# An encoder trunk on one core: first bias sums in a free buffer, later bias loads behind the stacks, gates stored through GpSimd's queue

## The chip, the core and the metric

The kernel runs on one core of one Trainium2 chip. A core has TensorE (matmuls, PE in the profile, with its weight loads as PEld), VectorE (DVE), ScalarE (ACT), GpSimd (POOL) and SyncE (SP, which only starts transfers). The metric is the device time of one execution in microseconds; the time of a kernel is the median of several runs.

## The reference

Two layers of an encoder over 512 tokens of width 1024. Each layer is a feed-forward half-step, a mixer with three attention branches, and a second feed-forward half-step. The change lies in the mixer:

```python
u = rmsnorm(h, mix_pre_g[l])
proj = u @ w_in[l]
qa, ka, va, qb, kb, vb, qc, kc, vc, gl = jnp.split(proj, split_at, axis=-1)
oa = neighbourhood_attention(qa, ka, va, na_rpb[l])          # branch A, 8 heads
ob = sliding_window_attention(qb, kb, vb, sw_sink[l])        # branch B, 8 heads, 2 key heads
oc = differential_attention(qc, kc, vc, lam, lam_init, ...)  # branch C, 4 heads
yb = jnp.einsum('bsnc,ncd->bsnd', stack([oa, ob, oc]), w_branch[l])
gates = jax.nn.sigmoid(gl.reshape(b, s, 3, D_MODEL) + b_gate[l])
merged = jnp.sum(gates * yb, axis=2)
h = h + rmsnorm(merged @ w_out[l], mix_post_g[l])
```

In branch A each head has its own table of biases by relative position, which are added to the scores, and a mask for the columns outside the window:

```python
bias = rpb[:, dr[:, None, :, None], dc[None, :, None, :]]
scores = scores + bias[None].astype(jnp.float32)
scores = jnp.where(col_ok[None, None, None, :, None, :], scores, NEG)
p = jax.nn.softmax(scores.reshape(b, h, rows, GRID_W, kr * GRID_W), axis=-1)
```

## The kernel before

All is float32. Matmuls are done on operands split into a high and a low part, three matmuls for a product. A layer has four phases, each with a pool of SBUF tiles of its own: feed-forward, projection (`project`), mixer (`mixer`), feed-forward. The pools of consecutive phases use the same memory, so a tile of the mixer's pool can be written when the projection's tiles under it are done with. Other tiles live in a pool for the whole program (`sb`), with a fixed number of buffers for each tag: the tag `n` has two buffers of 128 x 2048 floats.

`project` computes the queries, keys and values. Most of them it stores to DRAM as high and low parts (`part`, `store`, line 1405, on GpSimd's queue); those of the first pair of heads of branch A stay in SBUF, in tiles named `early`. In its loop over groups, at group 6, it calls `tables_of_a`: the three masks of branch A and the bias tables of heads 0 and 1 are loaded into one buffer of the tag `n`, the tile `pre`. The other buffer of that tag is then free until the first gates.

`mixer` works through steps that the text `ORDER` names, in that order:

- `qa0` to `qa3` load what a pair of heads of branch A needs (`qkv_a`). `ask` starts the load of a head's bias table (`braw`, line 1726; nothing to load for heads 0 and 1). `restacked` starts 12 loads of 128 KB that put high and low parts of queries and keys on top of each other (`st`, lines 1776 and 1777), and `values` two loads of values (`x`, line 1753). All are on SyncE's queue.
- `aa0` to `aa3` are the attention of such a pair (`attn_a`). For each head, `biases` adds the mask to shifted views of the bias table, four additions on VectorE (line 1737), into two tiles, `bedge` and `bmid`, of the mixer's tag `g`, which has ten buffers. `softmax_pv` computes the scores (line 1672), adds the bias and takes the maximum in one operation of VectorE (line 1675), takes the exponential (line 1684) and scales (line 1692) on ScalarE, transposes (line 1703), splits the result (lines 352 and 353) and multiplies it with the values (lines 1706 and 1707).
- `kb`, `qb`, `ab` and `qc`, `ac`, `fc` are the loads and attention of branches B and C.
- `ga`, `gb`, `gc` with a number 0 to 7 each compute 128 of 1024 gates of a branch: 24 matmuls (lines 326 to 328) and a tanh (line 1909). Gates of branch A stay in SBUF, four in one buffer of the tag `n`; the first four take the buffer that is free beside `pre`, the next four that of `pre`. Gates of B and C go through two buffers of the tag `gd` and are stored to DRAM (line 1912, SyncE's queue).
- `ya`, `yb`, `yc` multiply a branch with its output weights and apply the gate (`combine`): gates of B are loaded back into `gd` buffers, the product with the gate is line 1922 on VectorE, the sum over branches line 1926, for branch B on GpSimd.

Weights come in blocks of 512 KB (`wr`, line 211), whose loads ScalarE starts in the mixer, and are split into high and low parts on ScalarE and VectorE (lines 224 and 225). Two PSUM banks (`mm`) take the products of gates and combine steps in turn.

Outside some regions that are ordered by hand, a scheduler lays down each engine's instructions when the program is built: it goes by the order in which the steps are written and by modelled times, and it picks which buffer of a tag a tile gets. On the chip each engine and each queue then works strictly in that order; whoever must wait holds up all that stands behind it.

Of the kernel before, what the change touches and what calls it, by code (L numbers as in the profile page):

```python
# [10 lines left out]
F32 = mybir.dt.float32  # L11
# [5 lines left out]
P = 128  # L17
# [3 lines left out]
T = 512  # L21
# [18 lines left out]
QA, KA, VA, QB, KB, VB, QC, KC, VC, GL = 0, 4, 8, 12, 16, 17, 18, 22, 26, 30  # L40
# [29 lines left out]


ORDER = """
qa0 qa1 aa0 ga0 ga1 qa2 aa1 ga2 qa3 aa2 ga3 gb0 kb qb0 aa3 gb1 qb1 ab0
gb2 gb3 qb2 ab1 gb4 gb5 gb6 qb3 ab2 gb7 ga4 qc0 ab3 ga5 ga6 qc1 ac0
ga7 ya0 gc0 ya1 qc2 fc0 ac1 gc1 ya2 gc2 ya3 gc3 fc1 qc3 ac2 ya4 ya5
ya6 ya7 yb0 gc4 fc2 ac3 yb1 gc5 yb2 gc6 fc3 yb3 gc7 yb4 yb5 yb6 yb7
yc0 yc1 yc2 yc3 yc4 yc5 yc6 yc7
# [42 lines left out]
def encoder_kernel(ctx: ExitStack, tc: tile.TileContext, order, xT, wts, cols, rows, rpb, consts, tables, out):  # L120
    nc = tc.nc
# [3 lines left out]
    sb = ctx.enter_context(tc.tile_pool(name="sb", bufs=1))  # L125
# [4 lines left out]
    BUFS = {"X": 6, "n": 2, "wr": 3, "wp": 2, "wq": 2}  # L130
# [16 lines left out]
    def nm(s):  # L147
        serial[0] += 1
        return f"{s}{serial[0]}"

    def big(tag, dt=F32, shape=(P, T), name="v"):
        if tag in BUFS:
            return sb.tile(list(shape), dt, tag=tag, name=nm(name), bufs=BUFS[tag])
        kind, pool = phase[0]
        return pool.tile(list(shape), dt, tag=tag, name=nm(name), bufs=ABUFS[kind][tag])
# [7 lines left out]
    V, A, G, PE = nc.vector, nc.scalar, nc.gpsimd, nc.tensor  # L163

    def f(t):
        return t.bitcast(F32)
# [15 lines left out]
    def col(name, l, b=0, t=None):  # L182
        c = COLS[name, l] + b
        return (colt if t is None else t)[:, c : c + 1]
# [76 lines left out]
    for l in range(L):  # L261
        for which in (1, 2):
            name = f"ffn{which}_w_down"
# [81 lines left out]
    def dense1(name, l, c, X, r0=0, tag="mm", midway=None):  # L345
        return dense([(name, l, r0, c)], X, (tag,), midway=midway)[0]
# [1021 lines left out]
    def project(l, op, accs):  # L1368
# [112 lines left out]
        made = {}  # L1481
# [38 lines left out]
        for n, c0 in (("cosR", 0), ("sinR", 512)):  # L1520
            t = big("rr", name=n)
# [25 lines left out]
        def tables_of_a():  # L1547
            t = sb.tile([P, 4, T], F32, tag="n", name=nm("pre"), bufs=BUFS["n"])
            nc.sync.dma_start(t[:, 0, :], tables[:, 1024 : 1024 + 512])
            nc.sync.dma_start(t[:, 1, :256], tables[:, 1024 + 512 : 1024 + 768])  # L1550
            for hd in range(2):
                nc.sync.dma_start(t[:, 2 + hd, :], raw_of(l, hd))
            made["tables"] = t

        def gate_tile(c):
            if (c - GL) % 4 == 0:
                made["gates"].append(sb.tile([P, 4, T], F32, tag="n", name=nm("gate"), bufs=BUFS["n"]))
            return made["gates"][-1][:, (c - GL) % 4, :]
# [19 lines left out]
        for g in range(count):  # L1578
# [48 lines left out]
            if g == 6:  # L1627
                tables_of_a()
# [6 lines left out]
    def raw_of(l, hd):  # L1635
        return bass.AP(rpb.tensor, (l * 8 + hd) * 16 * RPBW, [[RPBW, 8], [1, 16], [1, 8 * RPBW]])
# [77 lines left out]
    def mixer(l, op, made):  # L1714
# [6 lines left out]
        def ask(hd):  # L1721
            if hd < 2:
                raws[hd] = pre[:, 2 + hd, :]
                return
            raw = raws[hd] = big("g", name="braw")
            nc.sync.dma_start(raw, raw_of(l, hd))

        def biases(hd):
            raw = raws.pop(hd)
            edge = big("g", name="bedge")  # L1730
            mid = big("g", shape=(P, 2 * P), name="bmid")

            def put(dst, mask, n0, n1):

                src = raw[:, 7 * RPBW + 39 - 8 * n0 :]
                (ps0, pn), _ = src.ap
                V.tensor_tensor(
                    out=dst.rearrange("p (d r c) -> p d r c", r=8, c=8),
                    in0=bass.AP(src.tensor, src.offset, [[ps0, pn], [-8, n1 - n0], [-RPBW, 8], [-1, 8]]),
                    in1=mask.rearrange("p (d r c) -> p d r c", r=8, c=8),  # L1740
                    op=ALU.add,
                )

            put(edge[:, 0:256], masks[0], 0, 4)
            put(mid, masks[1], 0, 4)
            put(edge[:, 256:384], masks[2][:, :P], 2, 4)
            put(edge[:, 384:512], masks[2][:, P:], 0, 2)
            return lambda i: edge[:, 0:256] if i == 0 else edge[:, 256:512] if i == NT - 1 else mid


        def load(d, dt=F32, tag="tx"):
            x = big(tag, dt, name="x")
            nc.sync.dma_start(f(x), d)
            return x
# [12 lines left out]
        def restacked(c, both):  # L1767
            if c in (QA, KA):
                return made[c]
            hi, lo = made[c]  # L1770
            res = []
            for s in range(2):
                own, pair_ = slice(64 * s, 64 * s + 64), []
                for one, two in ((hi, lo), (lo, hi))[: 2 if both else 1]:
                    st = big("st", F32R, name="st")
                    nc.sync.dma_start(f(st)[0:64], one[own])
                    nc.sync.dma_start(f(st)[64:128], two[own])
                    pair_.append(st)
                res.append((pair_ + [None])[:2])
            return res  # L1780

        def values(c):
            t = made[c] if c == VA else [load(d, F32R, "st") for d in made[c]]
            if c >= VC:
                return t
            v = [x.rearrange("p (b h d) -> p b h d", b=2, h=2) for x in t]
            return lambda j, s: v[j // 2][:, j % 2, s, :]
# [11 lines left out]


        def qkv_a(p):
            for s in range(2):
                ask(2 * p + s)
            return restacked(QA + p, False), restacked(KA + p, True), values(VA + p)

        oa = [sb.tile([P, 4, T], F32R, tag="X", name=nm("oa"), bufs=BUFS["X"]) for _ in range(2)]

        def attn_a(p, sq, sk, vof):
            o = big("t", name="o")
            for s in range(2):  # L1810
                rest = softmax_pv(
                    sq[s], sk[s], lambda j, s=s: vof(j, s), biases(2 * p + s), 1.0, None,
                    perm(o[64 * s : 64 * s + 64, :]), natural, SEEN_A,
                )
                follow(rest)

            def done():
                OT["a", p] = tuple(t[:, p, :] for t in oa)
                A.activation(OT["a", p][0], o, AF.Copy)
                V.tensor_tensor(out=OT["a", p][1], in0=o, in1=f(OT["a", p][0]), op=ALU.subtract)  # L1820

            pending.append(done)
# [80 lines left out]
        def gates(n, *ms):  # L1903
            for m in ms:
                pg = dense1(w, l, GL + n * KD + m, X)
                if n == 0 and m % 4 == 0:
                    gate0.append(sb.tile([P, 4, T], F32, tag="n", name=nm("gate"), bufs=BUFS["n"]))
                t = gate0[m // 4][:, m % 4, :] if n == 0 else big("gd", name="gate")
                A.activation(t, pg, AF.Tanh, scale=0.5, bias=col("b_gate", l, n * KD + m))
                if n:  # L1910
                    d = dr.tile([P, T], F32, tag="gate", name=nm("gate"), bufs=4 * KD)
                    nc.sync.dma_start(d, t)
                    t = d
                gate[n, m] = t

# [42 lines left out]
        def do(u):  # L1958
            kind, i = u[:2], int(u[2:] or 0)
            if kind == "fc" or kind[0] == "y":  # L1960
                if kind == "fc" and i >= len(oc) or kind[0] == "y" and (kind[1], 3) not in OT:
                    settle()
            if kind == "qa":
                held[u] = qkv_a(i)
            elif kind == "kb":
                tables_in()
                held["kb"] = qkv_b(KB), values(VB)
            elif kind == "qb":
                held[u] = qkv_b(QB + i)
            elif kind == "qc":  # L1970
                held[u] = qkv_c(i)
            elif kind == "aa":
                attn_a(i, *held.pop(f"qa{i}"))
            elif kind == "ab":
                attn_b(i, held.pop(f"qb{i}"), *held["kb"])
            elif kind == "ac":
                attn_c(*held.pop(f"qc{i}"))
            elif kind == "fc":
                finish_c(i)
            elif kind[0] == "g":  # L1980
                gates("abc".index(kind[1]), i)
            elif kind[0] == "y":
                combine("abc".index(kind[1]), kind[1], i)
# [78 lines left out]
    for l in range(L):  # L2062
        with open_phase("f"):
            X, accs = ffn(l, 1, X, accs)
        with open_phase("p"):
            made = project(l, X, accs)
        with open_phase("m"):
            X, accs = mixer(l, X, made)
        with open_phase("f"):
            X, accs = ffn(l, 2, X, accs)  # L2070
# [59 lines left out]
```

## Time and profile before

| | |
|---|---|
| median of 3 runs | 2384.1 us |
| lowest and highest | 2383.48, 2388.46 us |
| the profiled execution | 2380.2 us, its span 2378.4 us |
| TensorE busy | 2346.9 us (99%) |
| VectorE, ScalarE, GpSimd busy | 1883.2, 1448.5, 178.8 us |
| gate stores (line 1912) | 32 of 256 KB, from 552.5 to 1952.1 us |

The profile is one execution. The views used below are: the page (sums of the whole span), the busy time by stage (each engine's busy time in a stretch, then the granted clock of TensorE, the share of time that the 16 DMA engines were busy, and GB/s), the waits (who waited for whom, total us, times, longest), the timeline (start, duration, engine, line, operation, tiles out<-in, shapes, count, and in brackets the idle time before it and what ended it), the groups by line (busy us, mean ns, idle before), and the chain of waits that ended last. A q behind an engine's name marks its instruction queue. In the first layer the mixer begins at about 505 us, in the second at about 1683 us.

### The profile page before, as it was taken

The page shows a single profiled execution, that of the slowest core. Times are in us where ns is not written, and L with a number is a line of the kernel's source. Part 1 is how long each engine was busy: PE and PEld are TensorE (multiplying, and loading weights), DVE is VectorE, ACT ScalarE, POOL GpSimd, SP SyncE. Part 2 cuts the span into 40 slices and gives each one's busy share as a digit, 9 for nine tenths or more (in the row PEclk, how much of TensorE's full clock was granted, in tenths as well). Part 3 has the DMA queues.
Part 4 walks back from the last instruction along what each step waited for, and adds up shares of the span by engine and source line. Part 5 has one row for each costly group of instructions (what it writes and reads, how often), then busy time and mean ns, then how long its engine had stood idle before and what let it go on. Part 6 is the DMA issues. An engine that isn't in the chain of part 4 may idle for free. (4 is left out here: it accounts for less than half of the span.)

```text
span 2378.4 us, 39981 instructions
## 1 busy us (share of the span) xinstructions
PE 2346.9 (99%) x15062; PEld 2105.4 (89%) x15062; DVE 1883.2 (79%) x3056; ACT 1448.5 (61%) x2711; POOL 178.8 (8%) x242
## 2 busy tenths in 40 slices
PE   9999999999999999999999999999999999999998
PEld 8999889987888789998899998899878878899987
DVE  7887987967977577888878878889589766788796
ACT  6565566668766365655655554666687664556563
POOL 0111001110000101110001110011000010011100
PEclk9999999999999999999999999999999999999999
DMA  5566446667565534664525565376766664346642
GB/s 170 161 169 192 153 142 197 207 205 214 164 186 177 158 100 141 170 159 166 174 87 169 160 178 195 107 218 207 210 188 175 171 201 131 106 144 170 192 144 87
DMA packets 143264, 395.13 MB, mean 166 GB/s; under 512 B 19296, under 2 KB 26080, under 8 KB 142560
## 3 DMA queue, kind: packets, MB, share of 16 engines
q1 hardware_dynamic: 114672, 279.25, 37.8%
q0 software_dynamic: 12992, 57.68, 9.4%
q10 hardware_dynamic: 15408, 55.66, 7.7%
q8 instruction: 118, 1.93, 0.3%
q14 instruction: 74, 0.61, 0.1%
HBM read 326.98 MB, written 80.74 MB: 171 GB/s over the span
## 5 line engine op out<-in xcount | busy, mean ns | idle before, releaser
L680 PE MATMUL mm<-X,h 128*128 128x256 f32 x1472 | 261.6, 277 | 0.2
L224 ACT ACTIVATE w<-wr 128x512 fp32r<-128x512 f32 x272 | 167.7, 627 | 119.9 <-PE mm L328 67.9
L225 DVE TENSOR_TENSOR w<-wr,w 128x512 fp32r<-128x512 f32 x272 | 190.9, 710 | 59.7 <-ACT w L224 58.8
L326 PE MATMUL mm<-X,w 128*128 128x512 f32 (+1 forms) x602 | 228.5, 380 | 2.0 <-ACT X L553 1.8
L327 PE MATMUL mm<-X,w 128*128 128x512 f32 (+1 forms) x602 | 227.8, 378 | 0.8 <-DVE X L554 0.7
L328 PE MATMUL mm<-X,w 128*128 128x512 f32 (+1 forms) x602 | 226.4, 377 | 0.0
L680 PEld LDWEIGHTS mm<-X,h 128*128 128x128 f32 x1472 | 223.6, 188 | 1.2 <-DVE v L738 0.5
L680 PE MATMUL mm<-ht,l 128*128 128x256 f32 x736 | 205.9, 280 | 0.0
L680 PE MATMUL mm<-ht,h 128*128 128x256 f32 x736 | 205.5, 279 | 0.0
L680 PE MATMUL mm<-lt,h 128*128 128x256 f32 x736 | 204.8, 278 | 0.0
L680 PE MATMUL mx<-ht,h 128*128 128x256 f32 x736 | 203.7, 277 | 0.0
L680 PE MATMUL mx<-lt,h 128*128 128x256 f32 x736 | 203.6, 277 | 0.0
L680 PE MATMUL mm<-X,l 128*128 128x256 f32 x736 | 203.6, 277 | 0.0
L680 PE MATMUL mx<-ht,l 128*128 128x256 f32 x736 | 203.4, 276 | 0.0
L630 DVE TENSOR_TENSOR l<-wr,h 128x1024 fp32r<-128x1024 f32 x92 | 112.5, 1223 | 62.7 <-PE mm L680 62.6
L662 ACT ACTIVATE h<-wr 128x1024 fp32r<-128x1024 f32 x92 | 97.7, 1062 | 73.6 <-PE mx L680 52.6
L680 PE MATMUL at<-X,w 128*128 128x256 f32 x1104 | 141.1, 277 | 0.0
L680 PEld LDWEIGHTS mm<-ht,l 128*128 128x128 f32 x736 | 138.7, 188 | 0.1
L680 PEld LDWEIGHTS mm<-lt,h 128*128 128x128 f32 x736 | 138.7, 188 | 0.0
L680 PEld LDWEIGHTS mm<-ht,h 128*128 128x128 f32 x736 | 138.6, 188 | 0.0
L680 PEld LDWEIGHTS mx<-lt,h 128*128 128x128 f32 x736 | 138.3, 188 | 0.0
L680 PEld LDWEIGHTS mx<-ht,h 128*128 128x128 f32 x736 | 138.1, 188 | 0.2
(449 smaller groups left out, 6748.2 us busy)
## 6 DMA issues: line engine op xcount, KB each, us to landing
wr<-in_wts_dram SPq DMA_DIRECT2D x269, 512.0 KB
wr<-in_wts_dram ACTq DMA_DIRECT2D x106, 512.0 KB
sum<-in_wts_dram POOLq DMA_DIRECT2D x64, 512.0 KB, 4.9
st<-part SPq DMA_DIRECT2D x120, 128.0 KB
ap<-in_wts_dram SPq DMA_DIRECT2D x20, 512.0 KB
a<-kept SPq DMA_DIRECT2D x32, 256.0 KB
ap<-sum SPq DMA_DIRECT2D x16, 512.0 KB
x<-part SPq DMA_DIRECT2D x32, 256.0 KB
```

The lines of the kernel that those rows point to most:

```text
L224: A.activation(hi, raw, AF.Copy)
L225: V.tensor_tensor(out=lo, in0=raw, in1=f(hi), op=ALU.subtract)
L326: PE.matmul(acc, w[0], x[0], start=start, stop=False)
L327: PE.matmul(acc, w[0], x[1], start=False, stop=False)
L328: PE.matmul(acc, w[1], x[0], start=False, stop=stop)
L630: V.tensor_tensor(out=w["l1"], in0=self.raws[g][0], in1=f(w["h1"]), op=ALU.subtract)
L662: A.activation(self.W[g]["h24"], self.raws[g][1], AF.Copy)
L680: PE.matmul(acc, ws[i], xs[j], start=start and k == m == 0, stop=stop and k == n - 1 and m == 2, skip_group_check=True,)
```

## The change

Four edits. The bias sums of heads 0 and 1 go into a new tile `edges` that `tables_of_a` takes in the other buffer of the tag `n`; the first four gates of branch A get that buffer behind them. In the order, the first gates computed behind `aa0` are therefore two of branch B, and those of branch A follow from behind `aa1` on; one gate moves from behind `ab0` to behind `aa3`. `qkv_a` starts the loads of the stacks and values first and those of the biases behind them. The gates of B and C are stored through GpSimd's queue.

```diff
 ORDER = """
-qa0 qa1 aa0 ga0 ga1 qa2 aa1 ga2 qa3 aa2 ga3 gb0 kb qb0 aa3 gb1 qb1 ab0
-gb2 gb3 qb2 ab1 gb4 gb5 gb6 qb3 ab2 gb7 ga4 qc0 ab3 ga5 ga6 qc1 ac0
+qa0 qa1 aa0 gb0 gb1 qa2 aa1 ga0 qa3 aa2 ga1 ga2 kb qb0 aa3 ga3 gb2 qb1
+ab0 gb3 qb2 ab1 gb4 gb5 gb6 qb3 ab2 gb7 ga4 qc0 ab3 ga5 ga6 qc1 ac0
...
             made["tables"] = t
+            made["edges"] = sb.tile([P, 4, T], F32, tag="n", name=nm("edges"), bufs=BUFS["n"])
...
         def biases(hd):
             raw = raws.pop(hd)
-            edge = big("g", name="bedge")
-            mid = big("g", shape=(P, 2 * P), name="bmid")
+            if hd < 2:
+                edge = made["edges"][:, hd, :]
+                mid = made["edges"][:, 2, 2 * P * hd : 2 * P * (hd + 1)]
+            else:
+                edge = big("g", name="bedge")
+                mid = big("g", shape=(P, 2 * P), name="bmid")
...
         def qkv_a(p):
+            got = restacked(QA + p, False), restacked(KA + p, True), values(VA + p)
             for s in range(2):
                 ask(2 * p + s)
-            return restacked(QA + p, False), restacked(KA + p, True), values(VA + p)
+            return got
...
                     d = dr.tile([P, T], F32, tag="gate", name=nm("gate"), bufs=4 * KD)
-                    nc.sync.dma_start(d, t)
+                    G.dma_start(d, t)
```

## The prediction

> **What bounds the kernel now.** I read the page first, then the busy time by stage, the waits of TensorE in the two mixers, the queue of SyncE, and the chain of waits.
>
> ```profile
> span 2378.4 us, 39981 instructions
> ...
> PE 2346.9 (99%) x15062; PEld 2105.4 (89%) x15062; DVE 1883.2 (79%) x3056; ACT 1448.5 (61%) x2711; POOL 178.8 (8%) x242
> ```
>
> TensorE works for 2346.9 of 2378.4 us, and the change adds and removes no matmul. All that it can gain is idle time of TensorE, 31.5 us in the whole kernel, and of that only what lies in the mixers. The busy time by stage (first PE, then weight loads, DVE, ACT, POOL; behind them clock, DMA share, GB/s) says how much: attention A with its gates and the start of B is 505 to 600 us in layer 0 and 1683 to 1775 in layer 1; the combine steps and attention C are the other two rows.
>
> ```profile
> 505.00:600.00 95.00, 91.03 (x510) 75.54 (x510) 68.33 (x223) 75.05 (x210) 2.14 (x4) 1.00 0.72 203
> ...
> 690.00:800.00 110.00, 107.03 (x503) 86.72 (x502) 76.67 (x157) 65.27 (x123) 11.94 (x8) 0.98 0.63 189
> 1683.00:1775.00 92.00, 88.48 (x489) 73.14 (x488) 67.14 (x221) 73.19 (x204) 2.14 (x4) 1.00 0.73 209
> ...
> 1868.00:1980.00 112.00, 107.98 (x506) 87.38 (x505) 77.36 (x156) 64.62 (x120) 11.93 (x8) 0.98 0.61 185
> ```
>
> The A stages leave 4.0 and 3.5 us idle, the combine stages 3.0 and 4.0. What TensorE waited for in the two A stages (total us, times, longest), and, in the last row, in the combine steps of both layers:
>
> ```profile
> PE o L1707 <- DVE lo L353: 1.9, 2, 1.5
> PE at L1703 <- ACT s L1692: 1.5, 1, 1.5
> PE o L1706 <- ACT hi L352: 0.3, 1, 0.3
> ...
> PE at L1703 <- ACT s L1692: 1.3, 1, 1.3
> PE o L1707 <- DVE lo L353: 1.0, 2, 0.7
> PE mx L1672 <- DMA st<-part: 0.7, 1, 0.7
> PE o L1706 <- ACT hi L352: 0.3, 1, 0.3
> ...
> PE mm L326 <- DVE x L1922: 4.9, 3, 2.3
> ```
>
> The seven rows of the A stages sum to 7.0 us. That is the prize, 0.3% of the kernel; a measurement of this kernel can tell about 0.2%, or 4.8 us, from no change.
>
> **The bias sums of the first two heads.** They go from the mixer's pool, which lies over the projection's tiles, into a buffer that is free since the projection began.
>
> ```profile
> 507.69 0.72 PE L1672 MATMUL mx<-early 128*128 128x256 f32 x4
> 514.90 0.43 DVE L1737 TENSOR_TENSOR bedge<-pre 128x256 f32<-128x256 f32 x1 [2.35 <-DMA part<-lo]
> L1737 DVE TENSOR_TENSOR bedge<-pre 128x128 f32<-128x128 f32 (+1 forms) x12 | 3.6, 332 | 3.5 <-DMA part<-lo 3.5
> ```
>
> The first scores stand in PSUM from 508.4 us, and their softmax begins only behind the bias sum of 514.90, which waited for the last store of the projection. The sums themselves stay (same 16 operations); the wait of 3.5 us in both layers goes, and VectorE's softmax can begin 6.5 us earlier. On TensorE this is worth nothing directly: no wait of it in the A stage of layer 0 lies ahead of 535 us, since gate matmuls cover it. It is a head start of 6.5 us for the chain of attention A.
>
> **The next biases asked behind the stacks.**
>
> ```profile
> SPq L1726 <- DMA part<-hi: 53.6, 2, 27.4
> 486.14 28.83 SPq L1726 DMA_DIRECT2D braw<-in_rpb_dram  x2
> 515.07 0.51 SPq L1776 DMA_DIRECT2D st<-part  x1
> ```
>
> SyncE's queue stands for 27.4 us (53.6 in both layers) in front of the second bias load of pair 1, whose buffer the projection's last store holds. Queued behind it are the 12 stack loads and 2 value loads of that pair. With the biases behind them, these start when their own buffers are free: somewhere between 486.8 us and now. Here is what their lateness costs:
>
> ```profile
> 510.00:515.00 5.00, 5.00 (x24) 4.14 (x23) 0.79 (x2) 3.00 (x4) 0.97 (x2) 1.00 0.50 199
> 525.00:530.00 5.00, 5.00 (x29) 4.29 (x28) 4.14 (x12) 3.39 (x10) 0.00 (x0) 1.00 0.88 197
> 530.00:535.00 5.00, 5.00 (x32) 4.32 (x31) 4.60 (x20) 3.23 (x11) 0.00 (x0) 1.00 0.95 207
> 535.00:540.00 5.00, 3.54 (x21) 2.76 (x20) 1.51 (x6) 3.69 (x13) 0.00 (x0) 1.00 0.85 250
> ...
> 536.31 0.51 ACT L1692 ACTIVATE s<-s,l 128x256 f32<-128x256 f32 x1 [3.09 <-DMA wr<-in_wts_dram]
> ...
> 1639.91 4.06 DMA wr<-in_wts_dram
> 1702.48 9.45 DMA wr<-in_wts_dram
> ```
>
> Two pairs' loads pile up behind 515 us and the DMA engines are 88 to 95% busy. A weight load of 512 KB that takes 4.06 us elsewhere takes 9.45 us here (both rows from the chain of waits, layer 1). ScalarE issues those loads itself, and its next issue stands until the last has landed: ScalarE loses 3.09 us, and TensorE's wait for the scaled probabilities, 1.5 and 1.3 us, is this same wait. If part of the pile moves ahead of 515 us, where the share is 0.50, the weight load shortens and these 2.8 us go. At best a load of 4.06 us removes all of it; at worst the pile stays, and nothing goes. I take the full 2.8, because it is the nearer end: ScalarE needs only 3.1 of the 9.45 us back. The wait of 0.7 us for a stack goes too, since that load no longer queues behind a bias load. What may come late instead is the bias of pair 1:
>
> ```profile
> L1737 DVE TENSOR_TENSOR bedge<-braw,pre x36: 260/287/426, 528.2 to 1732.6; 128x128 f32<-128x128 f32 x24, 128x256 f32<-128x256 f32 x12
> ```
>
> Its first use is at 528.2 us. If its load goes out 2 to 4 us behind today's 515 and lands as slowly as 9.45 us, it is just in time. I cost it at nothing; if that cover is gone, it costs about the 1 us by which it misses.
>
> The waits for L1706 and L1707, 3.5 us over both layers, sit late in the stage, where a step of attention ends with few gate matmuls left. The head start could remove them or the new order could enlarge them: from -3.5 to +3.5, and I take 0.
>
> **The gates, reordered and stored through GpSimd's queue.**
>
> ```profile
> L1909 ACT ACTIVATE gate<-mm,colt x48: 672/686/691, 513.9 to 1951.4; 128x512 f32<-128x512 f32 x48
> gate<-gate SPq DMA_DIRECT2D x32, 256.0 KB
> SPq L1912 <- ACT gate L1909: 81.0, 18, 10.6
> 508.64 0.54 POOL L1405 DMA_DIRECT2D part<-hi  x1 [6.94 <-ACT hi L1410]
> part<-hi POOLq DMA_DIRECT2D x30, 256.0 KB, 4.0
> ```
>
> 48 gates are computed before and after, 686 ns each on ScalarE, so the swap of ga0, ga1 for gb0, gb1 costs TensorE and ScalarE nothing in itself. Thirty-two stores leave SyncE, which stood 81.0 us in front of them with loads queued behind; GpSimd pays 0.54 us for each, 17 us in all, on an engine that is 8% busy. Queued behind them on GpSimd are the 16 additions of L1926; a store goes out some 4.5 us ahead of the next addition (775.34 and 779.81 in the rows of the combine steps below), so I cost that at nothing, and at up to 1 us an addition if a store stands too late. A store by that queue lands after 4.0 us. What remains is that two stores, 512 KB, now fall into the crowded 515 to 535 us; that is the slower rival below.
>
> **The combine steps.**
>
> ```profile
> 779.81 1.68 POOL L1926 TENSOR_TENSOR gate<-gate,x 128x512 f32<-128x512 f32 x1 [10.41 <-DVE x L1922]
> 775.34 0.33 SPq L1912 DMA_DIRECT2D gate<-gate  x1
> 781.51 5.12 SPq L1753 DMA_DIRECT2D x<-gate  x3
> 785.08 0.77 PE L326 MATMUL mm<-hi,w 128*128 128x512 f32 x1 [2.22 <-DVE x L1922]
> 785.00:788.50 3.50, 3.42 (x9) 2.74 (x10) 1.53 (x2) 0.00 (x0) 2.96 (x2) 0.53 0.45 140
> ```
>
> TensorE waits there for a PSUM bank, behind a gate load that SyncE issued at 781.51, the moment GpSimd's addition of 779.81 ended and freed its buffer. The buffer, not the store, set that time, and the two buffers stay two. I take 0. The ends: -4.9 us, with another 1.65 us (0.47 of 3.5 us) a layer because the clock fell to 0.53 behind the wait, which makes -8.2; or one more such wait, +3.9.
>
> **The sum** is 1.5 + 1.3 + 0.7 = 3.5 us less. The profiled execution took 2380.2 us (its span and 1.8 around it) and would take 2376.7; it lies 3.9 under the median of the runs, 2384.1, which becomes 2380.6.
>
> **Rivals.** *Nothing moves* (2384.1). The stacks come from the same pool as the late bias buffer, and some will lie over the projection's last tiles too; the queue then stands in front of a stack load until about 514 us and the pile is as before. For it: the row of 53.6 us shows that buffers of this pool come free that late. Against it: twelve loads wait today behind one buffer, and the last store can hold only some of their six. The Trainium skill, "DMA: Bandwidth & Descriptors", section "Issuing engines are not separate DMA queues", gives the same result on its own ground: transfers started from SyncE, ScalarE or GpSimd share the same 16 engines, so another issuing engine saves issue time only; by that rule alone the time would be 2384.1. The row of 81.0 us speaks against it in part, since the queue lost waits, not issue time.
>
> *The head start carries through* (2377.1, and 2368.9 with the combine waits). All seven waits of the A stages go, 7.0 us, because the attention chain runs 6.5 us earlier against the same gate matmuls, longer than any single wait. Against it: the order on each engine is laid down when the program is built, and waits like the 1.5 us for L1707 come of that order. With the 8.2 us of the combine steps it is 15.2.
>
> *Slower* (2390.1): the early gate stores lengthen the weight load in the crowded stretch. 256 KB inside the 9.45 us at some 200 GB/s is 1.3 us; TensorE's wait of 1.46 us becomes 2.8. It decides at the length where the clock falls: behind 1.46 us it did not (1.00 in the row of 535 to 540 us), behind 2.22 us it did. Past that, 1.65 us come on top: 3.0 a layer, 6.0 in both. It needs the pile to stay where it is. By the Trainium skill, "TensorE: Matmul & The Clock Gate", Part 1, the clock falls only after an idle window of about 3.4 us, and this rival would cost 2.6 us, 2386.7, inside 0.2%; the 2.22 us of the trace contradict that here, and the measurement decides.
>
> **How the numbers follow.** Forecast 0.38; head start carried through 0.22, with the combine waits 0.08; nothing moves 0.15; slower 0.17. Faster by over 0.2% are the two head-start cases and the part of the forecast (0.08) in which some of the late waits go as well: 0.38. Within 0.2%: the rest of the forecast and nothing moves, less 0.01 for an unlucky combine wait: 0.44. Slower: 0.18. The range, 2370 to 2390.5, reaches from just above the case with the combine waits (0.08 left out) to the slower one, of which the half that also meets a combine wait is left out. The forecast's own range is 2377 to 2384.
>
> **What would show it.** Right: VectorE's first bias sum of a mixer lies ahead of the scores, stack loads are issued ahead of 514 us, the DMA share of the stretch behind 515 us is lower, ScalarE's gap of 3.09 us in front of L1692 is gone, and the wait for L1706 and L1707 is about as it was. Wrong: SyncE stands some 27 us in front of a stack load; the weight load still takes over 9 us; waits for L1707 or L1922 that are larger than now; a third stretch at half clock.

## The result and the profile after

The changed kernel takes 2389.96 us (median of 18 runs, 2384.71 to 2397.51), the kernel before in the same runs 2384.19 (18 runs, 2379.39 to 2388.74). The ratio is 1.0027, 95% interval 1.0017 to 1.0038: slower by 5.8 us. The profiled execution took 2387.8 us, against 2380.2.

The page's first lines of the changed kernel:

```profile
span 2386.0 us, 39991 instructions
...
PE 2347.9 (98%) x15062; PEld 2104.9 (88%) x15062; DVE 1879.8 (79%) x3056; ACT 1442.2 (60%) x2707; POOL 197.9 (8%) x274
```

The span is 7.6 us longer and TensorE is busy for only 1.0 us more; 6.6 us are new idle time of TensorE. The busy time by stage says where (stages of layer 1 begin about 7 us later than before):

```profile
505.00:600.00 95.00, 94.53 (x530) 80.32 (x529) 67.97 (x217) 76.30 (x210) 5.38 (x10) 1.00 0.76 211
640.00:690.00 50.00, 46.42 (x214) 36.94 (x212) 36.19 (x80) 29.62 (x60) 1.08 (x2) 0.97 0.63 170
690.00:800.00 110.00, 102.39 (x476) 81.39 (x477) 74.24 (x155) 61.87 (x121) 15.88 (x14) 0.97 0.60 179
1690.00:1782.00 92.00, 89.88 (x491) 75.62 (x489) 61.79 (x202) 71.90 (x196) 5.38 (x10) 0.98 0.72 203
```

Attention A has won what there was to win in layer 0: 0.5 us idle instead of 4.0 between 505 and 600 us. The loss comes behind it, from 640 us on: 3.6 us idle in 50 us, and 7.6 instead of 3.0 between 690 and 800. Before, TensorE had no idle time at all in the first of these stretches:

```profile
600.00:690.00 90.00, 90.00 (x470) 75.99 (x469) 79.24 (x204) 64.85 (x152) 0.00 (x0) 1.00 0.56 163
```

What TensorE waited for in the mixers of the changed kernel:

```profile
PE at L363 <- DVE msc L1948: 8.1, 4, 2.9
PE o L1708 <- DVE lo L353: 4.3, 3, 2.5
PE mx L1863 <- ACT e L1870: 3.7, 2, 1.9
...
PE mx L1673 <- DVE nmx L1676: 1.9, 1, 1.9
...
PE at L1886 <- DVE nm L1866: 1.7, 2, 1.2
```

The rows named by the prediction for the scaled probabilities, for a stack and for the combine step (L1922 before) are gone. In their place stand others. Those of lines 363, 1863 and 1886 lie in attention C: 14.4 us with a row of 0.9 us that is not shown, where the kernel before had 1.9 us. The wait for the split of line 353 is as old as the kernel, but its longest now comes at 653 us, where there was none. The row of line 1673 is a wait for a late bias, in layer 1 (below). The first row is the spread of `finish_c` (line 363), which waits for the reciprocal of four numbers per partition, `msc`. The order of VectorE around the second longest of its four waits, from the timeline:

```profile
686.13 0.16 DVE L1901 TENSOR_SCALAR msc<-at 128x4 f32<-128x4 f32 x1 [1.48 <-PE at L1899]
686.21 0.68 DVE L225 TENSOR_TENSOR w<-wr,w 128x512 fp32r<-128x512 f32 x1
690.62 0.69 DVE L1767 TENSOR_TENSOR x<-x,cosR 128x512 f32<-128x512 f32 x1 [3.73 <-DMA sh<-raw]
691.23 0.17 DVE L1948 RECIPROCAL msc<-msc 128x4 f32<-128x4 f32 x1
```

This reciprocal takes 0.17 us, and ScalarE has its operand ready at 687.5 us (the square root, 0.21 us from 687.29). It stands behind the first rope product of the next query or key (line 1767), and that one waits 3.73 us for its load. VectorE works in order, so TensorE waits 2.6 us for the reciprocal. The wait of 2.5 us at 653 us has the same form, with a split in the reciprocal's place:

```profile
654.32 0.69 DVE L1767 TENSOR_TENSOR x<-x,cosR 128x512 f32<-128x512 f32 x1 [3.07 <-DMA x<-raw]
...
655.00 0.41 DVE L353 TENSOR_TENSOR lo<-at,hi 128x256 fp32r<-128x256 f32 x1
```

The load of the rope product at 690.62 us in turn was started late by SyncE (timeline, its queue):

```profile
668.66 3.33 SPq L1766 DMA_DIRECT2D sh<-raw  x4
681.37 1.11 SPq L1645 DMA_DIRECT2D st<-hi  x2
...
683.81 0.58 SPq L1758 DMA_DIRECT2D x<-raw  x1
684.50 3.11 SPq L1766 DMA_DIRECT2D sh<-raw  x4
```

From about 672 to 681 us SyncE stands in front of the first stack of the previous rope tile (L1645), and the next rope loads are queued behind it. The waits of SyncE's queue, before and after, fit a reading in which this stand took the place of the one that the change removed:

```profile
SPq L1644 <- ACT hi L352: 90.1, 16, 8.0
...
SPq L1912 <- ACT gate L1909: 81.0, 18, 10.6
```

```profile
SPq L1645 <- ACT hi L352: 173.1, 16, 23.6
```

Before, 81.0 + 90.1 = 171.1 us of standing; after, 173.1 in one place. SyncE no longer waits for gates, reaches the stacks earlier, and waits there as long. On VectorE the groups by line show the rope products waiting longer for their loads (last column: idle time ahead of them), first before, then after:

```profile
L1763 DVE TENSOR_TENSOR sh<-sh,sinR 128x512 f32<-128x512 f32 x16 | 11.0, 690 | 8.2 <-DMA sh<-raw 8.2
L1762 DVE TENSOR_TENSOR x<-x,cosR 128x512 f32<-128x512 f32 x16 | 11.0, 687 | 3.8 <-DMA x<-raw 3.7
```

```profile
L1767 DVE TENSOR_TENSOR x<-x,cosR 128x512 f32<-128x512 f32 x16 | 11.0, 686 | 18.5 <-DMA x<-raw 12.6 <-DMA sh<-raw 5.9
```

12.0 us of it before, 18.5 after. That the time was lost there is read; why those loads and products stood as they did had to be tried.

### The profile page after: what moved, and what is told of

Same layout as the page of the kernel before. It is cut to its first block, busy times and chain, and to the rows that moved or that the text cites. A ratio compares the mean times of both kernels' runs of the same rounds, so it can differ in the third digit from the quotient of the medians.

```text
span 2386.0 us, 39991 instructions
## 1 busy us (share of the span) xinstructions
PE 2347.9 (98%) x15062; PEld 2104.9 (88%) x15062; DVE 1879.8 (79%) x3056; ACT 1442.2 (60%) x2707; POOL 197.9 (8%) x274
## 5 line engine op out<-in xcount | busy, mean ns | idle before, releaser
L225 DVE TENSOR_TENSOR w<-wr,w 128x512 fp32r<-128x512 f32 x272 | 187.8, 699 | 64.4 <-ACT w L224 63.4
L680 PEld LDWEIGHTS mm<-X,l 128*128 128x128 f32 x736 | 138.3, 188 | 0.1
```

The costliest lines, as they stand in the source:

```text
L225: V.tensor_tensor(out=lo, in0=raw, in1=f(hi), op=ALU.subtract)
L680: PE.matmul(acc, ws[i], xs[j], start=start and k == m == 0, stop=stop and k == n - 1 and m == 2, skip_group_check=True,)
```

## The experiments

Three theories. **Q**: storing gates through GpSimd's queue does the harm itself, by late stores or by their load on the transfers. **H**: the head start of attention A shifts all later work against the gates, and attention C pays. **Z**, later **O**: each edit re-lays the order that the scheduler writes for every engine and queue, and it is that order that costs; with its mechanism, **B**: short steps stand, on VectorE, behind rope products whose loads are late. All ratios are against the kernel before, run beside them on the same chip. The kernels were timed in several rounds on different chips, so those of different rounds are compared by these ratios and not by their medians.

### The edits one by one

Gate stores through GpSimd alone:

```diff
-                    nc.sync.dma_start(d, t)
+                    G.dma_start(d, t)
```

> Only the gate stores move to GpSimd's queue. Theory Q (the store queue: gates that GpSimd stores free their buffers later, the laid-out order changes around the combine steps, and rope loads and the running-max stage of attention C come late): slower than before, about +5 us, 2388 to 2391, with TensorE waits at L363 in attention C that before does not have. Theory H (the head start of attention A moves all later steps against the gates, and the stage of attention C pays): no difference, 2383 to 2386. Theory Z (nothing in the C stage is due to one edit; every edit re-lays the order and the late waits fall out one way or the other): a change of either sign up to about 8 us, and waits in other places than after's.

All of the change without that edit:

```diff
-                    G.dma_start(d, t)
+                    nc.sync.dma_start(d, t)
```

> All of the change but the gate stores, which stay on SyncE's queue. Theory Q: the 7.0 us of the A stages are won and nothing is lost later, about 2377 to 2380. Theory H: as the changed kernel, about 2390, with the same waits at L363 and L1863/L1708 in attention C. Theory Z: anything between 2372 and 2392, with the A stages' waits gone in any case.

Only the biases asked behind the stacks:

```diff
+            got = restacked(QA + p, False), restacked(KA + p, True), values(VA + p)
             for s in range(2):
                 ask(2 * p + s)
-            return restacked(QA + p, False), restacked(KA + p, True), values(VA + p)
+            return got
```

> Only the bias loads move behind the stacks and values. By the prediction's step this takes the stretch behind 515 us apart: the 1.5 + 1.3 us of TensorE's wait behind the weight load and the 0.7 us for a stack go, about 2380.6. By the rival that nothing moves: 2384, SyncE standing some 27 us in front of a stack load. Theory Z: the A stage as one of these two says, but the C stage's waits changed by up to several us.

The free buffer with the new order of the gates, biases asked first, stores on SyncE; against the kernel of the second run:

```diff
-            got = restacked(QA + p, False), restacked(KA + p, True), values(VA + p)
             for s in range(2):
                 ask(2 * p + s)
-            return got
+            return restacked(QA + p, False), restacked(KA + p, True), values(VA + p)
```

> The bias sums in the free buffer together with the new order of the gates, without the two other edits. If the head start alone empties the A stages, their idle time falls from 4.0 and 3.5 us to under 1.5 each although the biases are still asked first. Theory H: the C stage's waits are there as in the changed kernel, total 2386 to 2391. Theory Q: they are not, 2377 to 2381.

The free buffer and the biases behind the stacks, with the old order of the gates and stores on SyncE; against the same:

```diff
-qa0 qa1 aa0 gb0 gb1 qa2 aa1 ga0 qa3 aa2 ga1 ga2 kb qb0 aa3 ga3 gb2 qb1
-ab0 gb3 qb2 ab1 gb4 gb5 gb6 qb3 ab2 gb7 ga4 qc0 ab3 ga5 ga6 qc1 ac0
+qa0 qa1 aa0 ga0 ga1 qa2 aa1 ga2 qa3 aa2 ga3 gb0 kb qb0 aa3 gb1 qb1 ab0
+gb2 gb3 qb2 ab1 gb4 gb5 gb6 qb3 ab2 gb7 ga4 qc0 ab3 ga5 ga6 qc1 ac0
```

> Bias sums in the free buffer and biases asked behind the stacks, with the old order of the gates and all stores on SyncE. If the new order of the gates is what lets the head start be used: slower than the kernel with all three of these edits (2374.4) by 3 us or more. If the two edits in attention A carry it alone: within 2 us of that kernel. The single edit of asking the biases later cost 8 us by itself; if that cost is the late bias sums of the first pair, it is gone here.

| kernel | median us | ratio | 95% interval |
|---|---|---|---|
| changed kernel | 2389.96 | 1.0027 | 1.0017 to 1.0038 |
| stores through GpSimd alone | 2387.65 | 1.0032 | 1.0021 to 1.0043 |
| biases behind the stacks alone | 2389.56 | 1.0039 | 1.0028 to 1.0051 |
| free buffer + gate order | 2383.50 | 1.0015 | 1.0005 to 1.0025 |
| free buffer + biases behind | 2396.26 | 1.0061 | 1.0048 to 1.0075 |
| free buffer + gate order + biases behind | 2374.42 | 0.9970 | 0.9957 to 0.9982 |

The last row is the change without its store edit: it is faster than before by 0.30%. So the store edit costs 0.57%, or 13.6 us, in company, and 0.32% alone. Theory H falls: the head start is all there in the last row, and attention C has no wait for `msc`. The longest waits of that kernel's mixers:

```profile
PE o L1708 <- DVE lo L353: 6.1, 2, 4.0
...
PE o L1890 <- DVE lo L353: 1.4, 1, 1.4
```

With the store edit alone the place differs, and the expected waits at L363 are only 1.2 us. The longest wait still reads the same way. First VectorE, then TensorE (timelines):

```profile
689.22 0.69 DVE L1762 TENSOR_TENSOR x<-x,cosR 128x512 f32<-128x512 f32 x1 [4.17 <-DMA x<-raw]
689.83 0.68 DVE L1922 SCALAR_TENSOR_TENSOR gate<-gate,mm 128x512 f32<-128x512 f32 x1
```

```profile
690.56 0.79 PE L326 MATMUL mm<-X,w 128*128 128x512 f32 x1 [2.90 <-DVE gate L1922]
```

A rope product waits 4.17 us for its load, a combine step behind it frees a PSUM bank late, and TensorE waits 2.9 us for that bank.

The three other edits carry each other. Biases asked later, alone, made the kernel slower, where the prediction's step had given a gain. Its first bias sum, which the prediction showed at 514.90 us, is now laid behind the split weights (timeline of VectorE):

```profile
526.01 0.69 DVE L225 TENSOR_TENSOR w<-wr,w 128x512 fp32r<-128x512 f32 x1 [2.60 <-ACT w L224]
526.62 0.42 DVE L1737 TENSOR_TENSOR bedge<-pre 128x256 f32<-128x256 f32 x1
```

Without that edit, the free buffer and the gate order leave SyncE's queue as it was, its first load of the pile at 514.55 us, and the earlier attention runs into its own loads (waits of that kernel):

```profile
PE mx L1673 <- DMA st<-part: 11.8, 4, 4.6
```

With the free buffer and the biases behind, at the old gate order, the kernel is slower than before by 0.61%, 14.5 us, and its rope products wait 33.6 us for their loads. That its first gates of branch A then need the buffer that holds the bias sums is argued from the code, not shown.

### Order or queue

The order that a program was built with can be compared row by row. Of the 32 gate stores, the first two of branch B in each layer (gb0, gb1) decide it: with these four on GpSimd the order of TensorE and ScalarE is that of the changed kernel to the row, VectorE's but for 4 rows at most; with them on SyncE and the other stores of branch B on GpSimd it is that of the 2374.42 us kernel to the row. So each theory can be given the same order with another queue.

```diff
-                    G.dma_start(d, t)
+                    (G if n == 1 and m < 2 else nc.sync).dma_start(d, t)
```

> The changed kernel with only 4 of its 32 gate stores left on GpSimd's queue: the first two of branch B in each layer (gb0 and gb1); the other 28 are back on SyncE. Built, it has the instruction order of the changed kernel on TensorE and ScalarE, row for row, and on VectorE but for 4 rows. Theory O (the order that the scheduler lays down is the cost, and it is these two stores that tip it): the time of the changed kernel, 2387 to 2392 against a before of 2384, with the same waits at L363 and L1863. Theory Q (a store through GpSimd's queue is itself late or lengthens other transfers, in the C stage above all): 28 of 32 stores are gone, so about 2375 to 2379, as with all stores on SyncE.

```diff
+                    (G if n == 1 and m >= 2 else nc.sync).dma_start(d, t)
```

> The counterpart: gb0 and gb1 are stored by SyncE, the 6 other gates of branch B (12 stores in both layers) by GpSimd, those of C by SyncE. Built, it has the instruction order of the kernel with all stores on SyncE, row for row on TensorE, VectorE and ScalarE. Theory O: that kernel's time, 6 to 8 us below before, 2375 to 2378. Theory Q: slower than that kernel by 12/32 of 13.6 us, about 5 us: 2380 to 2383.

```diff
+                    (G if n == 1 else nc.sync).dma_start(d, t)
```

> All 16 gate stores of branch B on GpSimd, the 16 of branch C back on SyncE; order on TensorE and ScalarE as in the changed kernel, row for row. Theory O: the changed kernel's time, 2387 to 2392. Theory Q, in the form that the stores of C in the late stretch do the harm: 2377 to 2382; in the form that those of B do: 2387 to 2392.

```diff
+                    (G if n == 2 or m < 2 else nc.sync).dma_start(d, t)
```

> The changed kernel with 20 of 32 gate stores on GpSimd's queue: the 16 of branch C and gb0 and gb1 of branch B; the other 12 on SyncE. Order as in the changed kernel on TensorE, VectorE and ScalarE, row for row. If the stores of branch C through GpSimd's queue cost something of their own (the kernel with those of C on SyncE stood at 1.0008 of before, the changed kernel at 1.0027): 1.0027 or more, 2387 to 2392 for a before of 2384. If only the order counts and those differences are spread: 1.0008 to 1.0025.

| order of | stores on GpSimd's queue | ratio | 95% interval |
|---|---|---|---|
| changed kernel | 32 | 1.0027 | 1.0017 to 1.0038 |
| changed kernel | 20 (C, gb0, gb1) | 1.0025 | 1.0016 to 1.0034 |
| changed kernel | 4 (gb0, gb1) | 1.0017 | 1.0005 to 1.0028 |
| changed kernel | 16 (B) | 1.0008 | 0.9999 to 1.0017 |
| all but the store edit | 12 (B without gb0, gb1) | 0.9981 | 0.9972 to 0.9990 |
| all but the store edit | 0 | 0.9970 | 0.9957 to 0.9982 |

Twenty-eight stores taken off GpSimd's queue change the time by 0.10%, four more, which tip the order, by another 0.47%. Of the two kernels with 16 and 12 stores there, which also differ by these four and the order, the difference is smaller, 0.27%: the one with 16 came out at 1.0008, where theory O had forecast the changed kernel's time. All four kernels of the one order still lie above both of the other, so theory O has most of it. No run has the changed kernel's order with all stores on SyncE, so what those four stores cost by themselves is not measured; that it is little is argued from the place of the waits. The waits for `msc` lie more than 100 us behind the stores of gb0 and gb1. First the waits of the kernel with 4 stores on GpSimd's queue, then with 12:

```profile
PE at L363 <- DVE msc L1948: 6.7, 4, 2.7
PE mx L1863 <- ACT e L1870: 3.6, 2, 2.4
```

```profile
PE o L1708 <- DVE lo L353: 5.7, 2, 4.3
```

The first has the waits of the changed kernel in attention C, the second has none of them, with three times the stores on GpSimd. A share of the queue is left possible: at the changed kernel's order the two kernels with branch C's stores on GpSimd stand at 1.0027 and 1.0025, the two with them on SyncE at 1.0017 and 1.0008; the intervals of the extremes just touch.

### The reciprocal ahead of the rope product

If the reciprocal's place is what costs, it can be moved alone: the root of the reciprocal is the reciprocal of the root, so it can stand right behind the mean.

```diff
                 V.tensor_scalar(out=ms, in0=tot[:, :NT], scalar1=1.0 / P, scalar2=EPS, op0=ALU.mult, op1=ALU.add)
+                V.reciprocal(out=ms, in_=ms)
                 totc.append(ms)
...
             A.activation(totc[hd], totc[hd], AF.Sqrt)
-            V.reciprocal(out=totc[hd], in_=totc[hd])
```

> The changed kernel, with the reciprocal of finish_c (0.17 us on VectorE, line 1948) taken ahead of the square root instead of behind it, so that it stands ahead of the rope product that waits for its load (3.73 us at 686.9 in the changed kernel). Otherwise the order of the changed kernel but for some 20 rows of TensorE. Theory B (VectorE, working in order, holds the reciprocal behind a rope product whose load is late, and TensorE waits at L363): the waits for msc (8.1 us in the changed kernel) go to under 1 us, and the time falls by 4 to 8 us to 2382 to 2386, that is 0 to 0.1% from before. Rival (TensorE's order there simply has too few fillers, so that the next wait takes its place): within 2 us of the changed kernel, the idle time at L1863, L1886 or L326 instead.

Measured 2378.45 us, ratio 0.9982 (0.9970 to 0.9993). Eight operations of 0.17 us, moved by one to three places, are worth 0.45%, or 10.7 us, more than the 4 to 8 us expected. They did not move quite alone: some 26 matmuls and 12 operations of ScalarE, all in attention C and the steps beside it, changed their order too, and how much of the 10.7 us is theirs is not separated. Its groups by line and its longest wait in the mixers:

```profile
L1767 DVE TENSOR_TENSOR x<-x,cosR 128x512 f32<-128x512 f32 x16 | 11.0, 687 | 18.9 <-DMA x<-raw 14.7 <-DMA sh<-raw 4.3
...
L1902 DVE RECIPROCAL msc<-msc 128x4 f32<-128x4 f32 x8 | 1.4, 176 | 0.2
```

```profile
PE o L1708 <- DVE lo L353: 4.1, 2, 2.4
```

The rope products wait as long as in the changed kernel, 18.9 us; but the reciprocal is no longer behind them, and the wait for `msc` has gone from the view altogether. The split of line 353 still stands behind such a product, and TensorE still waits 4.1 us for it. The rival, that another wait would take the place of the one for `msc`, falls. The same kernel with 28 of its stores back on SyncE, at the same order:

```diff
-                    G.dma_start(d, t)
+                    (G if n == 1 and m < 2 else nc.sync).dma_start(d, t)
```

> The kernel with the early reciprocal (0.9982 of before), with 28 of its 32 gate stores back on SyncE, at the same order of TensorE, VectorE and ScalarE, row for row. If the queue costs something of its own: lower than 0.9982 by 0.001 to 0.002, 2373 to 2377 for a before of 2381. If only the order and the late reciprocal counted: within 0.1% of 0.9982.

Measured 2377.81 us, ratio 0.9984 (0.9971 to 0.9997), beside 0.9982. With the late reciprocal out of the way the queue of the 28 stores makes no difference that these runs can tell.

### The loads themselves

The 2374.42 us kernel still had one wait of 4.0 us, at L1708. Timelines of its SyncE, VectorE and TensorE:

```profile
552.61 1.53 SPq L1766 DMA_DIRECT2D sh<-raw  x3
...
568.05 0.53 SPq L1918 DMA_DIRECT2D gate<-gate  x1
568.62 0.43 SPq L1766 DMA_DIRECT2D sh<-raw  x1
```

```profile
574.63 0.69 DVE L1768 TENSOR_TENSOR sh<-sh,sinR 128x512 f32<-128x512 f32 x1 [4.59 <-DMA sh<-raw]
```

```profile
576.50 0.58 PE L1708 MATMUL o<-lo,x 128*128 128x256 f32 x1 [3.99 <-DVE lo L353]
```

Three of four row blocks of a rope tile start at 552.61 us, the fourth 16 us later, behind the stacks of a pair and a gate store; the rope product waits 4.59 us for it and holds up the split that TensorE needs. One load a layer is moved:

```diff
-                nc.sync.dma_start(sh[32 * q : 32 * q + 32], made[c][32 * o : 32 * o + 32])
+                (G if q == 3 and c == QC else nc.sync).dma_start(sh[32 * q : 32 * q + 32], made[c][32 * o : 32 * o + 32])
```

> The kernel with all gate stores on SyncE (2374.4), with one load per layer moved to GpSimd's queue: the last of the four row blocks of the first rope tile of branch C, which SyncE there issued 16 us behind the other three (568.62 us), behind the stacks of a pair. If VectorE's stand of 4.59 us in front of that load is what TensorE waits for at L1708 (3.99 and 2.07 us in the two layers): both waits go, and the time falls by 5 to 7 us, to about 2368 to 2370. If the load is late for another reason (crowded DMA engines) or another wait takes its place: 2373 to 2376.

Measured 2371.32 us, ratio 0.9955 (0.9942 to 0.9968). That is below the kernel before by 0.45% and below the changed kernel by 0.72%, and the fastest of this study. Against its base, 0.9970, it is 0.15%, or 3.6 us, where 5 to 7 were expected, and the intervals overlap; the profiled spans, 2366.7 and 2374.0 us, are one execution each. Its rope products wait for 0.6 us in all, and the wait at L1708 is gone (4.1 us for a stack at L1673 stand in its place):

```profile
L1768 DVE TENSOR_TENSOR sh<-sh,sinR 128x512 f32<-128x512 f32 x16 | 10.9, 683 | 0.0
L1767 DVE TENSOR_TENSOR x<-x,cosR 128x512 f32<-128x512 f32 x16 | 10.9, 680 | 0.6 <-DMA x<-raw 0.6
```

Then all rope loads on GpSimd's queue, once in the 2374.42 us kernel and once in the changed one; both orders are re-laid by it.

```diff
-            x = load(made[c])
+            x = big("tx", name="x")
+            G.dma_start(f(x), made[c])
...
-                nc.sync.dma_start(sh[32 * q : 32 * q + 32], made[c][32 * o : 32 * o + 32])
+                G.dma_start(sh[32 * q : 32 * q + 32], made[c][32 * o : 32 * o + 32])
```

> The kernel with all gate stores on SyncE, with all rope loads of branch C (x and the four row blocks) on GpSimd's queue; this re-lays the order of every engine. If what harms are loads queued behind others on SyncE: 2366 to 2371. If the re-laid order decides: either side of 2374, up to 2388.

> The changed kernel with all rope loads of branch C on GpSimd's queue as well, behind its gate stores there; this re-lays the order. If the late rope loads on SyncE are the cause of the C stage's waits: the waits for msc go and the time is 2378 to 2383. If the order decides whatever the queue of these loads: 2386 to 2392.

Measured 2372.96 us (0.9966, 0.9952 to 0.9980) and 2381.48 us (0.9999, 0.9989 to 1.0009). Both have no wait for `msc`. The first is little better than its base (0.9970), a miss of the expected 2366 to 2371: a wait of 6.2 us in the combine steps (L1929) appears instead. The second wins back the loss of the changed kernel, with 10.8 us of rope products waiting in other places and 5.1 us in the combine steps. So the rope loads matter in the changed kernel; that the re-laid order gives part of it back each time is a reading of these waits and was not tried apart.

## Why the prediction was wrong, step by step

- **The bias sums in the free buffer**: right in kind, wrong in size. The wait of 3.5 us ahead of them is gone, the sums are done from 391.7 us on, in the projection. The softmax begins at 514.0 us instead of 516.0, so 2.0 us earlier and not 6.5: VectorE has the split of a weight (L225) laid ahead of it, which waits until 513.4 us for ScalarE.

```profile
L1742 DVE TENSOR_TENSOR edges<-pre x16: 278/351/419, 391.7 to 1586.7; 128x256 f32<-128x256 f32 x8, 128x128 f32<-128x128 f32 x8
L1676 DVE CUSTOM_DVE_ANT_0 s<-mx,edges x16: 418/424/426, 514.0 to 1701.7; 128x256 f32<-128x256 f32 x16
```

- **The biases behind the stacks**: right in company. Stack loads start at 501.8 us, as the prediction's marks wanted, ScalarE's gap of 3.09 us ahead of the scaling is gone, and so are TensorE's waits of 1.5, 1.3 and 0.7 us. These are the waits of the forecast's 3.5 us. One mark did not come: the DMA share behind 515 us is no lower (0.84 from 515 to 540 us, before and after), so that a shorter pile ended these waits is not shown. By itself the edit costs 0.39%, and the prediction, which took it as a step of its own, did not see that it needs the other edits. What it put at nothing, a bias that comes late, came in layer 1, with the last pair of heads: SyncE starts the loads at 1731.9 us, behind the pair's stacks, VectorE waits 2.08 us for one, and TensorE 1.9 us behind it (the row of line 1673 above). The kernel without the store edit has no such wait in layer 1.

```profile
1742.19 0.42 DVE L1742 TENSOR_TENSOR bedge<-braw,pre 128x256 f32<-128x256 f32 x1 [2.08 <-DMA braw<-in_rpb_dram]
```

- **The late waits of attention A** (lines 1706 and 1707 before), taken as unchanged, went in both layers; in layer 1 the late bias took their place.
- **The gates through GpSimd's queue**: this step failed. The prediction gives the 32 stores no term in its sum; of GpSimd's additions behind them it says "so I cost that at nothing", with a reserve of up to 1 us each. The view of the changed kernel puts no wait of TensorE in the mixers down to these additions. But with the stores of gb0 and gb1 on the other queue the scheduler laid another order in both mixers (some 750 of 15,062 matmuls stand elsewhere); why it did is not shown, presumably since it models SyncE as free earlier there. That order puts the reciprocal and a split (L353) behind rope products whose loads come late. Cost: 0.57% between the kernels with and without the edit, and 0.47% and 0.27% between two pairs of kernels that differ in order and by four stores. The prediction named waits that come of the order as an argument against a rival, and nowhere asked which short operation would stand behind which late load in attention C, where it costed nothing at all.
- **The combine steps**, taken as unchanged: the waits of 4.9 us for L1922 went, and came back as the last wait for `msc`. Here the reciprocal stands behind a combine step that waits 5.18 us for its gate:

```profile
785.36 0.69 DVE L1928 SCALAR_TENSOR_TENSOR x<-x,mm 128x512 f32<-128x512 f32 x1 [5.18 <-DMA x<-gate]
785.96 0.17 DVE L1948 RECIPROCAL msc<-msc 128x4 f32<-128x4 f32 x1
```

- **The rival on the slower side** had the sign and nearly the size (2390.1), by another mechanism, so its nearness is luck: it put the loss between 515 and 535 us, through a longer weight load. ScalarE has no such wait there now, and TensorE is busy for all of 510 to 540 us. Its half-clock term did come, elsewhere: four stretches of 3.4 us in the mixers where there were two (below).
- **Nothing moves** and its rule: the Trainium skill, "DMA: Bandwidth & Descriptors", section "Issuing engines are not separate DMA queues", says that another issuing engine saves issue time only. The runs agree as far as the queue itself goes with the early reciprocal (0.9984 and 0.9982 at the same order). As a forecast it failed: what changed the time was the order that came with the queue. Which loads stand behind which matters as well: the queue of a single 64 KB load decided a wait of 4.0 us.

## What to carry to other kernels

A scheduler's program has one order, and an edit of four transfers can re-lay some 750 of its 15,062 matmuls; cost such an edit by the order that it yields, and try the same order with and without the edit before blaming the queue. Look for short operations that feed the critical engine and stand, in order, behind one that waits for a load: the idle column of the groups by line finds them (18.5 us ahead of L1767), and moving eight reciprocals of 0.17 us, with the small shifts that came along, was worth 0.45% here, more than the three edits that helped (0.30%). A queue that stops waiting in one place and waits as long in the next has won nothing.

## What the runs showed of the hardware

TensorE's clock fell not by the length of a wait but by the idle time within fixed stretches of 3.4 us. The busy time of the changed kernel in such stretches, two by two (PE busy first; clock third from the end):

```profile
652.20:655.60 3.40, 0.89 (x5) 0.42 (x4) 1.28 (x4) 0.63 (x1) 0.00 (x0) 1.00 0.31 64
655.60:659.00 3.40, 3.40 (x9) 2.72 (x10) 3.34 (x6) 1.23 (x2) 0.00 (x0) 0.50 0.51 147
689.70:693.10 3.40, 1.56 (x11) 1.50 (x12) 1.17 (x3) 0.55 (x1) 0.54 (x1) 1.00 0.80 233
693.10:696.50 3.40, 3.40 (x17) 2.81 (x16) 3.31 (x6) 2.83 (x5) 0.00 (x0) 1.00 0.00 0
1741.00:1744.40 3.40, 1.54 (x13) 1.35 (x12) 2.21 (x9) 1.60 (x7) 0.00 (x0) 1.00 0.55 144
1744.40:1747.80 3.40, 3.40 (x13) 2.48 (x12) 2.31 (x7) 3.11 (x9) 0.00 (x0) 0.51 0.94 260
```

A wait of 2.6 us at 688.9 us, cut in two by the boundary at 689.7, left the clock at 1.00; one of 1.9 us at 1741.2, within one stretch, halved it for the next. Here the turn lies near 1.85 us of 3.4; with the store edit alone a stretch with 1.72 us idle (533.4 to 536.8 us) did it too, so that it is no sharp bound. Counted in this way between 490 and 2000 us in every kernel of this document, each stretch at full clock with 1.86 us idle or more halved the clock for the next, and none with under 1.5 us did. The half-clock stretches at 655.6, 785.3 and 1744.4 us are 38.0 and 281.0 times 3.413 us apart. The Trainium skill, "TensorE: Matmul & The Clock Gate", Part 1, states such a free-running window of 3413 ns. It also says that the clock falls after at least one idle window; these rows contradict that, since 1.54 us of work in the stretch from 1741.0 us did not keep the clock up.
